# A decoder layer on one core: x pairs and squares ordered on two engines, the last gate chains cut into parts, four summed loads issued earlier

## The chip, the cores and the metric

The kernel runs on one core of a Trainium2 chip. The metric is the device time of one execution in microseconds (us), as the median of several. Five engines work side by side, each through its own list of instructions in order: PE (TensorE, matmuls; its weight loads are shown as PEld), DVE (VectorE), ACT (ScalarE), POOL (GpSimd) and SP (SyncE, which here only issues DMA transfers). They wait for each other through semaphores. PE accumulates in PSUM, which has eight banks of 128 x 512 float32.

## The reference

One layer of a decoder on x of 256 tokens by 2048, all in float32. A Griffin branch and a stick-breaking attention run in parallel from the same normed input, are gated and summed; a SwiGLU feed-forward of 5632 and a gated embedding follow.

```
h = rmsnorm(x, g_mix)
x_r, g_r, q, k, v, gate_r, gate_a = split(h @ w_in)       # 2816, 2816, then 5 x 2048
xc = causal_depthwise_conv(x_r)                           # width 4
r, i = sigmoid(xc @ w_rg_a + b_a), sigmoid(xc @ w_rg_x + b_x)   # 16 diagonal blocks of 176
a = exp(-8 * r * softplus(-lam));  u = sqrt(1 - a*a) * (i * xc)
hh[t] = a[t] * hh[t-1] + u[t]                             # scan along tokens
y_r = (gelu(g_r) * hh) @ w_rnn_out
y_a = stick_breaking_attention(headnorm(q), headnorm(k), v) @ w_attn_out
x = x + (sigmoid(gate_r) * y_r + sigmoid(gate_a) * y_a) @ w_o
g, u = split(rmsnorm(x, g_ffn) @ w_ffn_gu);  x = x + (silu(g) * u) @ w_ffn_down
x = x + sigmoid(rmsnorm(x, g_ple) @ w_ple_gate) * (p @ w_ple_proj)
```

## The kernel before

**Weights as a stream.** All weights lie packed in one array in the order of use. A plan lists 128 x 128 tiles by stage; `CHUNKS` cuts it into chunks of up to eight tiles (128 x 1024, 512 KB). Here w5, whi 5 and wlo 5 are the raw load and the two halves of chunk 5, numbered from 0 over the whole plan. `Stream.dma_to` issues a chunk's load on SP into one of four `p32` buffers. `Stream.split_to` makes two float32r halves: `whi` on ACT (a copy, L277), then `wlo` on DVE (weight minus whi, L278), each in one of four buffers. So a load waits for the split of the chunk four before it, and a split waits for PE to be done with the chunk four before it. Each float32 product is three matmuls, high x high, high x low, low x high: `prod` (L546 to L548) for token-major results, `mm3` (L458 to L460) for the block-diagonal gates, `wide`/`low` (L476, L480) for feature-major ones. A chunk in `prod` is 12 matmuls of 512 columns.

**Summed chunks.** In some groups (`group`) seven products stand for eight on 2 x 2 blocks. Their slots have string names. "11", "T1", "21" and "22" are loaded into tiles with the tag Q (26 of 128 x 1024) instead of `p32`; `summed` (L261, DVE) adds them in place for "T1" to "T4". The order of the recurrent output's group ("ro", 0) is `LONG`: 11, T1, 21, 4, 5, 22, 6, 7, 8, T2, and so on; these are chunks 142 to 151.

**Order.** A scheduler orders each engine's list from the program, dependences and priorities. `tc.issue_after(ins)` puts what is traced inside behind `ins` on the engine of `ins`, and on no other.

**Stages around the change.** (1) Head: eight x pairs (two 128-row tiles of x transposed each) are loaded; `norm_parts` scales each by g_mix and splits it (ACT then DVE, two of each, 128x256; L357 and L354); `norm_sq` squares it on ACT and adds into `acc0` on DVE. Beside this runs the first group, half of gate_r, from w_in. `later` ties both to the DVE split (`lo_ins`). (2) Recurrence: for p = 0 to 10, `rnn_g(p)` computes a pair of columns of g_r and its gelu, `rnn_conv` a pair of x_r, `rnn_gates(p)` the block-diagonal products and then a chain: two sigmoids, exp and tanh, sqrt, the scan and a split of y. Sigmoid, gelu, exp/tanh and sqrt need different function tables on ACT, each change one ACT_TABLE_LOAD. `decay_scales` computes per-channel constants, within p = 0. After p = 9 and p = 10 (`GATE_R_AT`) follows one `block` of gate_r, eight chunks, and its two sigmoids (`gate`). L800 then loads the table with log and exp. (3) The recurrent output ("ro", two groups), v, attention and the rest follow. (4) At the end ("pg", two groups) `embedded(g)` makes four products of p in PSUM, which wait in their banks for the sigmoid of the gate; the last part writes the output.

Of the kernel before, what the change touches and what calls it, by code (L numbers as in the profile page):

```python
# [2 lines left out]

# [7 lines left out]
AF = mybir.ActivationFunctionType  # L11
# [15 lines left out]
NPR = KR // 2  # L27
NPD = KD // 2
# [7 lines left out]
LONG = ["11", "T1", "21", 4, 5, "22", 6, 7, 8, "T2", 9, 10, 11, "T3", 12, 13, 14, "T4", 15, 16, 17, 18, 19, 20, 21]  # L36
TWO = (0, 1)
LAST_GROUP = ("pg", 1)
NEG = -1e30


def pairs_of(name):

    return (0, 1, 2) if name == "gu" else (0, 1)


def is_sum(x):

    return isinstance(x, str) or isinstance(x, tuple) and x[0] == "S"
# [14 lines left out]
C_XR, C_GR, C_Q, C_K, C_V, C_GTR, C_GTA = 0, 22, 44, 60, 76, 92, 108  # L64
# [17 lines left out]
GATE_R_AT = {9: 2, 10: 3}  # L82
# [95 lines left out]
PLAN = plan()  # L178
# [9 lines left out]
CHUNKS = []  # L188
# [9 lines left out]
    LAST.append(len(CHUNKS))  # L198


class Stream:


# [5 lines left out]
        self.raw, self.parts, self.after = {}, {}, {}  # L209

    def dma_to(self, n):
        n = min(n, len(CHUNKS))
        while self.n_dma < n:
            j = self.n_dma
            i, a, b = CHUNKS[j]
            c = P * (b - a)
            mode = PLAN[i][0][3] if PLAN[i][0][0] == "tok" else 0
            if is_sum(mode):
                if c:
                    t = self.quad()  # L220
                    self.raw[mode] = t
            else:
                t = self.p32.tile([P, 1024], F32, tag="w32", name=f"w32_{j}")
                self.raw[j] = t
            if c:
                src = self.w[OFFS[j]:OFFS[j] + P * c].rearrange("(p c) -> p c", p=P)
                self.nc.sync.dma_start(t[:, :c], src)
            self.n_dma += 1
            if j in self.after:
                self.after.pop(j)()  # L230
# [93 lines left out]
def tile_hybrid_block(ctx: ExitStack, tc: tile.TileContext, xT: bass.AP, x: bass.AP, pT: bass.AP,  # L324
                      prm: bass.AP, w: bass.AP, out: bass.AP):
    nc = tc.nc
# [10 lines left out]
    def tl(tag, dt=F32):  # L337
        cnt[0] += 1
        tag = "H" if tag in "CT" else "Q"
        n, c = NT[tag]  # L340
        return act.tile([P, c], dt, tag=tag, name=f"{tag}_{cnt[0]}", bufs=n)
# [8 lines left out]
    def tt(o, a, b, op):  # L350
        nc.vector.tensor_tensor(o, a, b, op)  # L351
# [4 lines left out]
    def actv(o, i, f, **kw):  # L356
        nc.scalar.activation(o, i, f, **kw)  # L357

    S_ = Stream(nc, w, p32, phl, lambda: tl("X"), 4, 3)
# [25 lines left out]
    def pc(base, j):  # L385
        return prm_sb[:, base + j:base + j + 1]
# [13 lines left out]
    for n in ("h", "l"):  # L400
        t = cst.tile([P, 512], F32R, tag=f"w1{n}", name=f"w1{n}")
# [138 lines left out]
    def tok(pairs, k, t):  # L540
        x = rhs(pairs, k)
        return x[:, t * P:t * P + P], x[:, 256 + t * P:384 + t * P]

    def prod(ps, x, wh, wl, start=False, stop=False, goes_on=False):

        nc.tensor.matmul(ps, x[0], wh, start=start, stop=False, skip_group_check=goes_on)  # L546
        nc.tensor.matmul(ps, x[0], wl, start=False, stop=False, skip_group_check=goes_on)  # L547
        nc.tensor.matmul(ps, x[1], wh, start=False, stop=stop, skip_group_check=goes_on)  # L548
# [118 lines left out]
    xc, xcs, gel, y, gtr, ysum, xsum = {}, {}, {}, [], [], {}, {}  # L667
# [26 lines left out]

    def rnn_g(p):
        g = from_x(C_GR, p, "T")
        actv(g, g, AF.Gelu_apprx_tanh)
        gel[p] = g

    def rnn_gates(p):  # L700
        i = S_.pos
        wts = S_.take(("rg", p))
        wts = [wts[x] for x in range(wts.n)]
        if PLAN[i + 1][0] == ("rg2", p):
            w2 = S_.take(("rg2", p))
            wts += [w2[x] for x in range(w2.n)]
        n = 0
        pss = []
        for _ in range(2):
            ps = psum()  # L710
            for e in range(2):
                ks = rg_k_tiles(2 * p + e)
                for x, k in enumerate(ks):
                    t = rhs(xcs, k)
                    mm3(ps[:, e * 256:e * 256 + 256], wts[n], t[:, :256], t[:, 256:], x == 0,
                        x == len(ks) - 1)
                    n += 1
            pss.append(ps)
        r, i_, a = tl("T"), tl("T"), tl("T")
        for e in range(2):  # L720
            s = slice(e * 256, e * 256 + 256)
            actv(r[:, s], pss[0][:, s], AF.Sigmoid, bias=pc(PC_BA, 2 * p + e))
        for e in range(2):
            s = slice(e * 256, e * 256 + 256)
            actv(i_[:, s], pss[1][:, s], AF.Sigmoid, bias=pc(PC_BX, 2 * p + e))
        for e in range(2):
            s = slice(e * 256, e * 256 + 256)
            actv(a[:, s], r[:, s], AF.Exp, scale=cA[:, 2 * p + e:2 * p + e + 1])
        for e in range(2):
            s = slice(e * 256, e * 256 + 256)  # L730
            actv(r[:, s], r[:, s], AF.Tanh, scale=cT[:, 2 * p + e:2 * p + e + 1])
        nc.vector.tensor_scalar(r, r, -1.0, 1e-30, ALU.mult, ALU.max)
        actv(r, r, AF.Sqrt)
        tt(i_, i_, xc[p], ALU.mult)
        stt(r, a, 1.0, r, ALU.add, ALU.mult)
        tt(i_, i_, r, ALU.mult)
        for e in range(2):
            s = slice(e * 256, e * 256 + 256)
            nc.vector.tensor_tensor_scan(r[:, s], a[:, s], i_[:, s], 0.0, ALU.mult, ALU.add)
        tt(r, r, gel[p], ALU.mult)  # L740
        y.append(split(r, "B"))
        if p in pairs_of("ro"):
            ysum[p] = half_sums(r)

    def block(c0, b, step=None):

        pss = [psum() for _ in range(2)]
        wt = S_.take(("blk", c0, b))
        for k in range(KD):
            if step is not None and k % 2 == 0:  # L750
                step()
            _, _, hi, lo, o = wt[4 * k]
            for t, ps in enumerate(pss):
                prod(ps, tok(xg, k, t), hi[:, o:o + 512], lo[:, o:o + 512], k == 0, k == KD - 1)
        return pss
# [1 line left out]
    def rs_x(t):  # L757
        return rstd_tok[:, t:t + 1]

    def gate(c0, b, tag, step=None):  # L760
        ts = [tl(tag) for _ in range(2)]
        for t, ps in enumerate(block(c0, b, step)):
            actv(ts[t], ps, AF.Sigmoid, scale=rs_x(t))
        return ts


    def later(f):

        def run():
            with tc.issue_after(S_.lo_ins.ins):  # L770
                f()
        return run

    def squares_x(i):
        return later(lambda: norm_sq(xt[i], acc0, i == 0))

    also = {2 * i - 3: later(next_xg) for i in range(2, NPD)}
    also.update({n: squares_x(i) for i, n in enumerate((2, 4, 6, 8, 10, 12, 13, 14))})
    pss = group(("gtr", 0), xg, None, None, also)[0]

    def scaled_gates():
# [6 lines left out]
    for p in range(2):  # L788
        rnn_conv(p, from_x(C_XR, p, "T", scaled_gates if p == 0 else None, scale=False))
    for p in range(NPR):  # L790
        rnn_g(p)
        if p + 2 < NPR:
            rnn_conv(p + 2, from_x(C_XR, p + 2, "T", scale=False))
        if p == 0:
            with tc.issue_after(S_.lo_ins.ins):
                decay_scales()
        rnn_gates(p)
        if p in GATE_R_AT:
            gtr.append(gate(C_GTR, GATE_R_AT[p], "C"))
    tc.keep_in_program_order(nc.scalar.preload_act_table_set("natural_log_exp_and_others"))  # L800

    def whole(at, pairs, sums, also=()):

# [8 lines left out]
    def xg_sums(p):  # L812
        h = tl("T")
        hi, lo = parts(xg[p])
        tt(pair(h), f32(hi), f32(lo), ALU.add)
        xsum[p] = half_sums(h)

    n = len(LONG)
    for g in range(2):
        also = {n - 2 + i: (lambda p: lambda: xg_sums(p))(p) for i, p in enumerate(pairs_of("v"))} if g else ()  # L820
        for i, c in enumerate(whole(("ro", g), y, ysum, also)):
            o = gtr[2 * g + i // 2][i % 2]
            tt(o, c, o, ALU.mult)
# [3 lines left out]
    for g in range(2):  # L827
        for i, c in enumerate(whole(("v", g), xg, xsum)):
            r = rs_x(i % 2)
            v = tl("B", F32R)  # L830
# [117 lines left out]
    at = {}  # L948
# [5 lines left out]
    def step():  # L954
        for f, hp in at.pop(slot[0], ()):
            f(hp)
        slot[0] += 1
# [27 lines left out]
    for g in range(2):  # L985
        for i, ps in enumerate(group(("ao", g), ost, None)[0]):
            c, m = gta[2 * g + i // 2][i % 2], mix_r[2 * g + i // 2][i % 2]
# [46 lines left out]
    for g in range(2):  # L1034
# [11 lines left out]
        for n, ps in enumerate(group(("wo", g), mix, msum, fold)[0]):  # L1046
            t, b = n % 2, 2 * g + n // 2
# [53 lines left out]
    def embedded(g):  # L1101
        def run():
            for b in range(2):
                w_ = S_.take(("tok", "pg", g, ("x", b)))[0]
                for t in range(2):
                    ps = psum()
                    for k in range(2):
                        s = slice(k * 512, k * 512 + 512)
                        prod(ps, tok(pts, k, t), w_[2][:, s], w_[3][:, s], k == 0, k == 1)
                    pp.append(ps)  # L1110
        return run

    for g in range(2):
        qs_, t_ = group(("pg", g), h3, sum3, also={len(SEVEN) - 3: embedded(g)})
        for n, (q, c, op) in enumerate(zip(qs_, ("11", "T3", "T1", "T3"), (ALU.add,) * 3 + (ALU.subtract,))):
            t, b = n % 2, 2 * g + n // 2
            c, ps, o = t_[c], pp.pop(0), tl("T")
            m = 512 if g == 0 or n < 3 else 256
# [69 lines left out]
```

## Time and profile before

| | us |
|---|---|
| median of 3 runs | 1893.24 (1893.03 to 1894.4) |
| profiled execution | 1895.76 |
| its span, first to last instruction | 1894.0 |
| first matmul of the stream / last matmul starts | 5.36 / 1885.66 |

The profile is of one execution. "Busy" counts an engine's instructions; matmuls are pipelined and their ends are modelled, so 0.39 us is shown for a matmul whose successor starts 0.227 us later. "Idle before <- X" names what ended an idle time. A line of the code can be a helper's, so L277, L278, L351, L354 and L357 stand for many places. The stretches around the change:

| stretch | us | PE busy | DVE busy | ACT busy | granted clock |
|---|---|---|---|---|---|
| head | 8 to 21 | 12.04 | 6.46 | 12.07 | 1.00 |
| head, on | 21 to 26 | 3.76 | 3.59 | 5.00 | 1.00 |
| block after p = 9 | 340 to 356 | 15.01 | 11.43 | 12.68 | 1.00 |
| gates and block of p = 10 | 356 to 394 | 38.00 | 20.96 | 25.76 | 1.00 |
| start of the recurrent output | 394 to 416 | 18.42 | 15.71 | 14.54 | 0.92 |
| attention to the last group but one | 450 to 1825 | 1375.00 | 1000.52 | 791.58 | 1.00 |
| middle of the last stage | 1825 to 1845 | 19.65 | 16.49 | 13.27 | 1.00 |

### The profile page before, as it was taken

Reading aid. Unit: us, or ns where it says so; the run is one execution under the profiler, and the core shown is the slowest. Engines: PE = TensorE matmul, PEld = TensorE weight load, DVE = VectorE, ACT = ScalarE, POOL = GpSimd, SP = SyncE. Lnnn points to the kernel's source line nnn. Section 1 sums busy time; section 2 is a strip of 40 time slices with the busy share of each in tenths; the row PEclk is TensorE's granted clock in tenths of the full one; section 3 lists DMA queues with packets and bytes.
Section 4 is the critical chain, followed back from the end, with each engine's and each line's share of the span. In section 5 each row is a group of like instructions: output and inputs, shape, how many; then the busy total and the mean of one; then the engine's idle time right before and its main releaser. Section 6 shows DMA issues by size and latency. Waiting matters only on the chain.

```text
span 1894.0 us, 24003 instructions
## 1 busy us (share of the span) xinstructions
PE 1877.4 (99%) x9000; PEld 1575.7 (83%) x9000; DVE 1378.1 (73%) x1649; ACT 1156.7 (61%) x1531; POOL 2.2 (0%) x9
## 2 busy tenths in 40 slices
PE   9999999999999999999999999999999999999998
PEld 7899989878888888888888888888888888888886
DVE  6688887666786566665578988866886688855776
ACT  6688888764455567666455766544664466543663
POOL 0000000000000000000000000000000000000000
PEclk9999999999999999999999999999999999999999
DMA  7556555565646654555666555476447646466554
GB/s 268 180 177 195 196 175 193 182 221 179 232 146 190 199 162 146 171 169 166 193 217 215 201 214 220 144 255 213 161 160 254 213 146 221 147 220 190 171 191 138
DMA packets 101925, 361.36 MB, mean 191 GB/s; under 512 B 11440, under 2 KB 12080, under 8 KB 101808
## 3 DMA queue, kind: packets, MB, share of 16 engines
q1 hardware_dynamic: 101664, 359.82, 56.9%
q8 instruction: 70, 1.15, 0.3%
q14 instruction: 47, 0.39, 0.1%
q10 hardware_dynamic: 144, 0.01, 0.0%
HBM read 357.69 MB, written 2.10 MB: 190 GB/s over the span
## 4 chain that ended last, share of the span: by engine, by line
PE 95%; ACT 2%; DVE 1%; DMA 1%; issue 1%; SPq 0%; DVEq 0%; ACTq 0%
PE ps L547 26%; PE ps L548 26%; PE ps L546 26%; PE ps L476 8%; PE ps L480 4%; PE ps L459 1%; PE ps L460 1%; PE ps L458 1%; ACT L357 1%; ACT H L357 1%; DMA w<-in_w_dram 1%; ACT whi L277 1%; PE ps L1071 1%; DVE wlo L278 0%; DVE H L351 0%
## 5 line engine op out<-in xcount | busy, mean ns | idle before, releaser
L278 DVE TENSOR_TENSOR wlo<-w,whi 128x1024 fp32r<-128x1024 f32 (+1 forms) x580 | 701.2, 1215 | 375.7 <-ACT whi L277 370.9
L277 ACT ACTIVATE whi<-w 128x1024 fp32r<-128x1024 f32 (+1 forms) x580 | 607.1, 1052 | 469.3 <-PE ps L548 410.6
L547 PE MATMUL ps<-wlo,Q 128*128 128x512 f32 x2223 | 867.9, 390 | 1.4 <-DVE wlo L278 1.3
L548 PE MATMUL ps<-whi,Q 128*128 128x512 f32 x2223 | 866.8, 390 | 0.0
L546 PE MATMUL ps<-whi,Q 128*128 128x512 f32 x2223 | 791.5, 392 | 5.7 <-ACT whi L277 5.3
L546 PEld LDWEIGHTS ps<-whi,Q 128*128 128x128 f32 x2223 | 416.7, 188 | 93.3 <-ACT whi L277 8.5
L547 PEld LDWEIGHTS ps<-wlo,Q 128*128 128x128 f32 x2223 | 417.8, 188 | 89.8 <-DVE wlo L278 4.8
L548 PEld LDWEIGHTS ps<-whi,Q 128*128 128x128 f32 x2223 | 417.7, 188 | 86.7
L277 ACT ACTIVATE whi<-Q 128x1024 fp32r<-128x1024 f32 (+1 forms) x177 | 182.5, 1032 | 137.3 <-PE ps L548 114.5
L278 DVE TENSOR_TENSOR wlo<-Q,whi 128x1024 fp32r<-128x1024 f32 (+1 forms) x177 | 210.2, 1189 | 53.4 <-ACT whi L277 53.2
L476 PE MATMUL ps<-Q,whi 128*128 128x512 f32 x704 | 170.7, 392 | 0.0
L476 PEld LDWEIGHTS ps<-Q,whi 128*128 128x128 f32 x704 | 128.8, 188 | 24.5
L351 DVE TENSOR_TENSOR H<-ps,H 128x512 f32<-128x512 f32 (+1 forms) x170 | 98.4, 609 | 25.2 <-PE ps L548 16.0
L261 DVE TENSOR_TENSOR Q<-Q,Q 128x1024 f32<-128x1024 f32 x76 | 92.8, 1221 | 1.2 <-DMA Q<-in_w_dram 0.3
L480 PEld LDWEIGHTS ps<-Q,wlo 128*128 128x128 f32 x704 | 90.4, 191 | 3.5
L480 PE MATMUL ps<-Q,wlo 128*128 128x256 f32 x704 | 91.5, 283 | 0.0
L357 ACT ACTIVATE H<-ps 128x512 f32<-128x512 f32 (+1 forms) x122 | 60.4, 516 | 48.0 <-PE ps L548 28.4
L357 ACT ACT_TABLE_LOAD x64 | 82.1, 1283 | 1.1
L351 DVE TENSOR_TENSOR H<-H,H 128x512 f32<-128x512 f32 (+2 forms) x107 | 63.3, 598 | 3.1 <-ACT H L357 2.6
L357 ACT ACTIVATE Q<-H 128x512 fp32r<-128x512 f32 x41 | 25.1, 625 | 26.5 <-DVE H L351 25.6
L460 PE MATMUL ps<-Q,wlo 128*128 128x256 f32 x140 | 39.6, 283 | 0.0
L459 PE MATMUL ps<-Q,whi 128*128 128x256 f32 x140 | 39.6, 283 | 0.0
(130 smaller groups left out, 855.0 us busy)
## 6 DMA issues: line engine op xcount, KB each, us to landing
w<-in_w_dram SPq DMA_DIRECT2D x558, 512.0 KB, 3.9
Q<-in_w_dram SPq DMA_DIRECT2D x98, 512.0 KB, 6.1
w<-in_w_dram SPq DMA_DIRECT2D x16, 448.0 KB, 3.3
H<-in_x_dram SPq DMA_DIRECT2D x8, 256.0 KB, 5.3
H<-in_xT_dram SPq DMA_DIRECT2D x7, 256.0 KB, 7.6
out_dram<-H SPq DMA_DIRECT2D x7, 256.0 KB, 5.1
w<-in_w_dram SPq DMA_DIRECT2D x4, 320.0 KB, 3.4
w<-in_w_dram SPq DMA_DIRECT2D x2, 256.0 KB, 3.0
```

The costliest lines, as they stand in the source:

```text
L261: self.nc.vector.tensor_tensor(r[o], r[o], r[a], ALU.add)
L277: self.hi_ins = self.nc.scalar.activation(hi[:, :c], t[:, :c], AF.Copy)
L278: self.lo_ins = self.nc.vector.tensor_tensor(lo[:, :c], t[:, :c], hi[:, :c].bitcast(F32), ALU.subtract)
L351: nc.vector.tensor_tensor(o, a, b, op)
L357: nc.scalar.activation(o, i, f, **kw)
L459: nc.tensor.matmul(o, wt[0], xl, start=False, stop=False)
L460: nc.tensor.matmul(o, wt[1], xh, start=False, stop=stop)
L476: nc.tensor.matmul(pss[e], wt[0], rhs(xs, k), start=(k == 0), stop=(k == n - 1))
L480: nc.tensor.matmul(pss[e][:, :256], wt[1], rhs(xs, k)[:, :256], start=False, stop=False)
L546: nc.tensor.matmul(ps, x[0], wh, start=start, stop=False, skip_group_check=goes_on)
L547: nc.tensor.matmul(ps, x[0], wl, start=False, stop=False, skip_group_check=goes_on)
L548: nc.tensor.matmul(ps, x[1], wh, start=False, stop=stop, skip_group_check=goes_on)
```

## The change

- `dma_order` sorts the issue of loads: a summed chunk of ("ro", 0) gets a place 4.5 chunks ahead of its own in the plan, and `DMA_UPTO` makes a request for n chunks include them.
- `later` becomes `behind_splits`: what is traced inside stands behind the latest whi split on ACT and the latest wlo split on DVE. It also holds `decay_scales`. The x pair and square are requested at other slots, mostly by turns.
- `rnn_gates` becomes a generator with four stops. For p = 9 and 10 its parts are traced before chunks 0, 2, 4 and 5 of the eight chunks of the following block (`count`), behind the splits and behind the gelu.
- The sigmoids of the last block go to slot 8 of ("ro", 0) (`last_gate`), the table load to slot 12 (`next_table`), both behind the splits.
- The four products of p for the first half of "pg" are copied by ACT from PSUM to SBUF.

```diff
+EARLY = {("ro", 0): 4}
...
+def dma_order():
+
+    def key(j):
+        k = PLAN[CHUNKS[j][0]][0]
+        early = k[0] == "tok" and is_sum(k[3]) and k[1:3] in EARLY
+        return j - (EARLY[k[1:3]] + 0.5 if early else 0)
+    order = sorted(range(len(CHUNKS)), key=key)
+    at = {j: n for n, j in enumerate(order)}
+    upto, m = [0], 0
+    for j in range(len(CHUNKS)):
+        m = max(m, at[j] + 1)
+        upto.append(m)
+    return order, upto
...
-        n = min(n, len(CHUNKS))
+        n = DMA_UPTO[min(n, len(CHUNKS))]
         while self.n_dma < n:
-            j = self.n_dma
+            j = DMA_ORDER[self.n_dma]
...
+        yield
         for e in range(2):
...
+    @contextmanager
+    def behind_splits():
+        with tc.issue_after(S_.hi_ins.ins), tc.issue_after(S_.lo_ins.ins):
+            yield
...
-            with tc.issue_after(S_.lo_ins.ins):
+            with behind_splits():
                 f()
...
-    also = {2 * i - 3: later(next_xg) for i in range(2, NPD)}
-    also.update({n: squares_x(i) for i, n in enumerate((2, 4, 6, 8, 10, 12, 13, 14))})
+    also = {max(1, 2 * i - 4): [later(next_xg)] for i in range(2, NPD)}
+    for i in range(NPD):
+        also.setdefault(2 * i + 1 if i < 7 else 14, []).append(squares_x(i))
...
-        rnn_gates(p)
-        if p in GATE_R_AT:
-            gtr.append(gate(C_GTR, GATE_R_AT[p], "C"))
-    tc.keep_in_program_order(nc.scalar.preload_act_table_set("natural_log_exp_and_others"))
+        parts_ = rnn_gates(p)
+        next(parts_)
+        if p not in GATE_R_AT:
+            list(parts_)
+            continue
+
+        count = [0]
+
+        def step():
+            if count[0] in (0, 2, 4, 5):
+                with behind_splits(), tc.issue_after(gelu.ins):
+                    next(parts_, None)
+            count[0] += 1
+
+        pss = block(C_GTR, GATE_R_AT[p], step)
+        if p < NPR - 1:
+            gtr.append(sigmoids(pss, "C"))
+        else:
+            pend_gtr = pss
...
+    def last_gate():
+        with behind_splits():
+            gtr.append(sigmoids(pend_gtr, "C"))
+
+    def next_table():
+        with behind_splits():
+            nc.scalar.preload_act_table_set("natural_log_exp_and_others")
...
-        also = {n - 2 + i: (lambda p: lambda: xg_sums(p))(p) for i, p in enumerate(pairs_of("v"))} if g else ()
+        also = {n - 2 + i: (lambda p: lambda: xg_sums(p))(p) for i, p in enumerate(pairs_of("v"))} if g else {
+            8: last_gate, 12: next_table}
...
+                    if g == 0:
+                        t_ = tl("T")
+                        actv(t_, ps, AF.Copy)
+                        ps = t_
                     pp.append(ps)
```

## The prediction

> **What bounds the kernel.** I read the page's busy times first, then who waited for whom on PE, the table of stretches, and last the timelines of PE, ACT and DVE where PE waited.
>
> ```profile
> span 1894.0 us, 24003 instructions
> ...
> PE 1877.4 (99%) x9000; PEld 1575.7 (83%) x9000; DVE 1378.1 (73%) x1649; ACT 1156.7 (61%) x1531; POOL 2.2 (0%) x9
> ```
>
> PE is the bound. The diff leaves the number of matmuls at 9000, so only time in which PE waits or runs slowly can be won. The waits on PE:
>
> ```profile
> PE ps L546 <- ACT whi L277: 5.3, 5, 1.8
> PE ps L588 <- DVE ones_r L398: 1.5, 1, 1.5
> PE ps L547 <- DVE wlo L278: 1.3, 3, 0.8
> PE ps L546 <- DVE H L351: 0.3, 1, 0.3
> ```
>
> Few, and all for a weight chunk's two halves (whi by ACT, wlo by DVE) or for DVE. A busy sum hides half of the loss, because a matmul's modelled 0.39 us overlaps the next. I therefore count from start to start: undisturbed 512-column matmuls start 0.227 us apart (408.57, 408.80, 409.03 in PE's timeline), a full chunk of 12 takes 2.72. Four places fall behind this.
>
> Head, ACT's timeline (start, length, operation):
>
> ```profile
> 15.81 0.89 ACT L357 ACTIVATE Q<-H,gm_sb 128x256 fp32r<-128x256 f32 x2
> 16.60 0.62 ACT L357 ACTIVATE H<-H 128x512 f32<-128x512 f32 x1
> ...
> 20.57 0.61 ACT L357 ACTIVATE H<-H 128x512 f32<-128x512 f32 x1
> 21.09 1.04 ACT L277 ACTIVATE whi<-w 128x1024 fp32r<-128x1024 f32 x1
> ```
>
> Four x pairs and squares in a row hold the next whi back to 21.09, though its weights landed at 18.70. Gate chain of p=9, PE's timeline:
>
> ```profile
> 345.44 0.42 PE L546 MATMUL ps<-whi,Q 128*128 128x512 f32 x1
> 346.62 0.50 PE L547 MATMUL ps<-wlo,Q 128*128 128x512 f32 x1 [0.76 <-DVE wlo L278]
> ```
>
> Start of the recurrent output, ACT, then PE:
>
> ```profile
> 392.71 1.06 ACT L277 ACTIVATE whi<-Q 128x1024 fp32r<-128x1024 f32 x1 [2.52 <-DMA Q<-in_w_dram]
> 396.40 2.01 ACT L277 ACTIVATE whi<-Q 128x1024 fp32r<-128x1024 f32 x2 [2.63 <-DVE Q L261]
> 398.42 1.28 ACT L357 ACT_TABLE_LOAD   x1
> 399.72 1.27 ACT L357 ACTIVATE H<-ps,rstd_tok 128x512 f32<-128x512 f32 x2
> 401.00 1.28 ACT L800 ACT_TABLE_LOAD   x1
> 402.30 1.06 ACT L277 ACTIVATE whi<-w 128x1024 fp32r<-128x1024 f32 x1
> ```
>
> ```profile
> 403.41 0.97 PE L546 MATMUL ps<-whi,Q 128*128 128x512 f32 x3 [1.83 <-ACT whi L277]
> ```
>
> The summed load lands late, and then the last gate's sigmoids with two table loads stand between two splits. Right after, the granted clock halves (stretch, PE, PEld, DVE, ACT, POOL, clock, DMA share, GB/s):
>
> ```profile
> 394.00:416.00 22.00, 18.42 (x69) 13.44 (x68) 15.71 (x14) 14.54 (x16) 0.00 (x0) 0.92 0.61 211
> 404.50:407.90 3.40, 3.23 (x8) 2.56 (x9) 2.99 (x4) 2.66 (x4) 0.00 (x0) 0.50 0.61 177
> ```
>
> Tail, PE:
>
> ```profile
> 1839.52 0.47 PE L546 MATMUL ps<-whi,Q 128*128 128x512 f32 x1 [0.35 <-DVE H L351]
> ```
>
> **x pairs and squares: -2.0.** The two chunks from 17.91 to 25.39 take 7.48 for 2 x 2.72 = 5.44: 2.04 lost. In the changed program's order each pair and square stands behind a split on ACT as well as on DVE. Walked with these rows: w4 lands 13.43, whi to 14.5; pair 2 to 15.35; the first square to 15.87; whi of w5 to 16.8 (0.9 later than before), its wlo to 18.1, wanted by PE at 18.83. Pair 3 to 17.6; w6, no longer behind the load of pair 6 (0.65 us at the 1.3 us per 512 KB of these landings), lands at 18.05, whi to 19.1, wlo (behind pair 3's low half) to 20.4; PE wants them at 20.6 and 21.5. Afterwards ACT needs per two chunks 2 x 0.95 + 0.8 + 0.6 = 3.3 us of PE's 5.44, DVE 3.8. The loads of pairs 6 and 7 move behind w9 and w10 on SP: about 23 and 25, asked for by ACT past 27 and 32. The wait for w2 near 8 us is the DMA's and stays.
>
> The decay scales' Abs and Exp leave the head and bring a table load of their own, 1.28 us. It lands in this hole of ACT, which it fits with its two 0.2 us neighbours:
>
> ```profile
> 98.27 0.66 ACT L357 ACTIVATE H<-ps 128x256 f32<-128x256 f32 x2 [2.42 <-PE ps L476]
> ```
>
> I take 0; were there no cover, the next whi (98.81, wanted by PE at 104.56) still has over 3 us. The Trainium skill, "ScalarE: Activation LUTs", section "What ACT_TABLE_LOAD costs", adds a drain of about 1.38 us to each load. Here the instruction behind a load starts 0.01 later (402.29 to 402.30), and with the drain the hole would overflow by 0.6, still under PE's cover. The total of loads stays 66 (p=9 saves one).
>
> **Chains of p=9 and p=10 in four parts: -2.0.** First matmuls of the gate's chunks stand at 342.72, 345.44, 349.27, 352.56 and 355.61; the last three steps are 3.83, 3.29 and 3.05 for 2.72: 2.01 lost. Before, whi of the chunk due at 345.44 ended at 345.31, behind four table loads. Now gelu comes first (no return to its table) and splits stand between parts: whi 339.8 to 340.85, wlo to 342.1; the following ones end whi 344.8, 345.8, 348.65 and wlo 346.05, 347.2, 350.3, for starts at 347.9, 350.6, 353.4. Delayed y is split at 352.9, used far later. Nothing waits.
>
> **Summed loads moved up, last sigmoids and table moved down: -6.7.** From the group's first matmul (394.84) to its eighth chunk (415.15) lie 60 matmuls (chunks 11, T1, 21, 4, 5, 22, 6): 20.31 for 13.6. What p=10's chain delays shows here too. The walk, as if the earlier savings had not shifted it: the four Q loads now issue behind w131; their buffers' last readers are gate matmuls of p=6 to p=9, done by 334.5, so SP does not stop. They add 4 x 1.3 = 5.2 us of transfer ahead of w132 to w134, landing about 359 to 362 (shifted by the 2 us of p=9), wanted by whi at about 359 to 364.5 because the split buffers free up only then. PE's margin over the finished splits: some 4 us. I charge 0.
>
> whi 11 then runs 386.8 to 387.9 instead of 392.71; DVE, solid from 390.4: wlo 11, y's low half, two sums (1.22 each), wlo T1 to 395.7, wlo 21 to 396.9, a third sum, wlo 4 to 399.2. PE asks for these at 396.4, 397.6 and 399.4; ACT's whi T1, 21, 4, 5 end 394.5, 395.4, 396.4, 398.0 for 396.0, 396.2, 398.7, 400.7. So covered, but by 0.2 to 0.7 only. The sigmoids (1.28 + 1.27) now follow the split of the eleventh chunk and the table load that of the fifteenth, where ACT is more than a chunk ahead; they hold two of eight PSUM banks and the group takes five. Bounds of this term: at least 3.9 (the 398.42 to 402.30 block leaves, loads late as before), at most 6.7.
>
> **Copies of the embedded products: -0.5.** Four ACT copies (0.58 each) near 1826 to 1830, where ACT's next split is wanted 7 us later; they free the bank for which PE lost 1839.52 - 1838.79 - 0.23 = 0.5. The end after the last matmul (1885.66 to 1894.02) keeps its order: 0.
>
> **Sum:** 2.0 + 2.0 + 6.7 + 0.5 = 11.2 against the profile's span of 1894.0 (1895.76 with what lies around it). That execution is 2.5 above the median of 1893.24; the waits are in both, so I take it off the median: 1882.0, and leave 0.5 for DVE's thin margin: **1882.5**.
>
> **Rivals.**
> 1. *The half clock does not belong to the waits and stays*: eight matmuls at 0.427 instead of 0.227, about 1.7 back: 1884.2. For: PE's longest idle before it is 1.83 us. Against: it is the only one after the warm-up, right behind the only cluster of waits. The Trainium skill, "TensorE: Matmul & The Clock Gate", Part 1, wants an idle window of about 3.4 us before the clock halves, which speaks for this rival; the trace shows no such idle, yet the clock fell.
> 2. *The loads do not land earlier, or DVE takes ACT's place*: only 3.9 of 6.7: 1893.24 - 8.4 = 1884.8. DVE's 0.2 us margin speaks for it, the free buffers against it.
> 3. *Given back elsewhere*: head and p=9 return their 4 (the late wlo of w5, say) and the output keeps 3.9: 4.4 left, 1888.8; a little more and it is no change.
> 4. *Slower: the four early loads starve the gates of p=10.* Eight loads follow w131 up to w135, four of them moved. If each took the 4.4 us that w131 took from issue to landing, one after another, w135 would land at 353.9 + 35.2 and be split 2.3 later for a PE that wants it at 373.6: 17.8 lost, net 6.6 slower, 1899.8. It outweighs the gains from (17.4 + 11.2) / 8 = 3.6 us per load. Against: five loads in a row landed 1.3 us apart at 392.6 to 397.7, and SP had free time.
>
> **Chances.** Forecast 0.60, rival 1 0.13, rival 2 0.13, rival 3 0.08 (half of it within 0.2%), rival 4 0.06. Runs of this kernel tell 0.2%, 3.8 us, from no change. The first three reach to 1885, rival 3 adds some: 1880.7 to 1887. Faster 0.90, same 0.04, slower 0.06.
>
> **What would show it.** Head: no ACT wait near 20; chunks 2.72 apart from 12 on. Gates: none near 345. Output: Q landed by 362, no table load between the splits of 21 and 4, seven chunks in about 13.6, granted clock 1.00. Tail: no wait for DVE H. Wrong if PE waits for wlo at the output's start, for w between 355 and 375, or anywhere new.

## The result, and the profile after

The changed kernel takes 1883.88 us, median of 4 runs (1883.51 to 1884.7), against 1893.82 for the kernel before beside it (1893.03 to 1895.63). The ratio is 0.9947, 95% interval 0.993 to 0.9964: 9.9 us less. The forecast was 1882.5 in 1880.7 to 1887.0. The profiled execution took 1884.7, its span fell from 1894.0 to 1883.0.

The waits on PE, changed kernel (engine and line that waited, who ended the wait: total, times, longest, in us):

```profile
PE ps L607 <- DVE ones_r L417: 1.5, 1, 1.5
```

Three of the four rows are gone. What stays is the start, before the stream's first matmul. (Lines have moved: L277 is now L296, L278 L297, L261 L280, L546 to L548 L565 to L567, and L357 L376.) The stretches, with the columns of the table before:

```profile
340.00:356.00 16.00, 16.00 (x72) 13.27 (x71) 12.00 (x15) 13.28 (x18) 0.00 (x0) 1.00 0.73 266
394.00:416.00 22.00, 22.00 (x99) 18.23 (x98) 15.67 (x15) 14.62 (x17) 0.00 (x0) 1.00 0.72 239
```

The start of the recurrent output held 69 matmuls in 22 us, now 99 do, at a clock of 1.00 for 0.92. ACT's timeline in the head and then at the recurrent output:

```profile
18.02 1.06 ACT L296 ACTIVATE whi<-w 128x1024 fp32r<-128x1024 f32 x1 [0.43 <-DMA w<-in_w_dram]
18.99 0.62 ACT L376 ACTIVATE H<-H 128x512 f32<-128x512 f32 x1
19.51 1.05 ACT L296 ACTIVATE whi<-w 128x1024 fp32r<-128x1024 f32 x1
20.46 0.89 ACT L376 ACTIVATE Q<-H,gm_sb 128x256 fp32r<-128x256 f32 x2
21.26 1.04 ACT L296 ACTIVATE whi<-w 128x1024 fp32r<-128x1024 f32 x1
```

```profile
383.04 1.06 ACT L296 ACTIVATE whi<-Q 128x1024 fp32r<-128x1024 f32 x1
...
389.63 2.01 ACT L296 ACTIVATE whi<-Q 128x1024 fp32r<-128x1024 f32 x2 [2.32 <-DVE Q L280]
391.55 1.04 ACT L296 ACTIVATE whi<-w 128x1024 fp32r<-128x1024 f32 x1
...
404.80 1.06 ACT L296 ACTIVATE whi<-w 128x1024 fp32r<-128x1024 f32 x1 [0.98 <-PE ps L567]
405.88 1.28 ACT L376 ACT_TABLE_LOAD   x1
407.17 1.27 ACT L376 ACTIVATE H<-ps,rstd_tok 128x512 f32<-128x512 f32 x2
```

In the head a pair or a square stands between two splits, never four of each. At the output the split of 11 is done at 384.10, 6.9 before PE starts that chunk at 391.00. The sigmoids stand where ACT is ahead.

PE place by place in the two profiled executions (the first row is a point in time, the next two are lengths, the last is time over the pace):

| place | before | after | gain | forecast |
|---|---|---|---|---|
| head: first matmul of chunk 7 at | 25.39 | 23.57 | 1.82 | 2.0 |
| chunks 124 to 131 (p = 9) | 23.794 | 21.787 | 2.01 | 2.0 |
| chunks 142 to 148 (recurrent output) | 20.31 | 13.60 | 6.71 | 6.7 |
| the wait for DVE near the end | 0.50 | 0 | 0.50 | 0.5 |

These sum to 11.04; the last matmul starts 11.01 earlier. Outside these places PE takes the same time in both to within 0.04 us.

### The profile page after: what moved, and what is told of

It reads as the page before. It is cut to its first block, busy times and chain, and to the rows that moved or that the text cites. A ratio compares the mean times of both kernels' runs of the same rounds, so it can differ in the third digit from the quotient of the medians.

```text
span 1883.0 us, 24009 instructions
## 1 busy us (share of the span) xinstructions
PE 1873.4 (99%) x9000; PEld 1576.0 (84%) x9000; DVE 1377.9 (73%) x1649; ACT 1158.5 (62%) x1535; POOL 2.2 (0%) x9
## 4 chain that ended last, share of the span: by engine, by line
PE 99%; DMA 0%; DVE 0%; SPq 0%; ACT 0%; issue 0%; DVEq 0%
PE ps L567 27%; PE ps L566 27%; PE ps L565 27%; PE ps L495 9%; PE ps L499 4%; PE ps L479 1%; PE ps L478 1%; PE ps L477 1%; PE ps L1127 1%; DMA w<-in_w_dram 0%; PE ps L919 0%; PE ps L1068 0%; DVE H L370 0%; PE ps L1030 0%; PE ps L973 0%; PE ps L972 0%
## 5 line engine op out<-in xcount | busy, mean ns | idle before, releaser
L297 DVE TENSOR_TENSOR wlo<-w,whi 128x1024 fp32r<-128x1024 f32 (+1 forms) x580 | 701.1, 1215 | 370.1 <-ACT whi L296 365.2
L296 ACT ACTIVATE whi<-w 128x1024 fp32r<-128x1024 f32 (+1 forms) x580 | 607.4, 1052 | 461.9 <-PE ps L567 402.4
L567 PE MATMUL ps<-whi,Q 128*128 128x512 f32 x2223 | 866.0, 390 | 0.0
L565 PE MATMUL ps<-whi,Q 128*128 128x512 f32 x2223 | 792.5, 392 | 0.0
L567 PEld LDWEIGHTS ps<-whi,Q 128*128 128x128 f32 x2223 | 417.4, 188 | 86.6
L565 PEld LDWEIGHTS ps<-whi,Q 128*128 128x128 f32 x2223 | 417.0, 188 | 85.5 <-ACT whi L296 0.8
L296 ACT ACTIVATE whi<-Q 128x1024 fp32r<-128x1024 f32 (+1 forms) x177 | 182.6, 1032 | 132.2 <-PE ps L567 112.3
L297 DVE TENSOR_TENSOR wlo<-Q,whi 128x1024 fp32r<-128x1024 f32 (+1 forms) x177 | 210.1, 1189 | 50.3 <-ACT whi L296 50.1
L280 DVE TENSOR_TENSOR Q<-Q,Q 128x1024 f32<-128x1024 f32 x76 | 92.8, 1221 | 0.9
L376 ACT ACTIVATE H<-ps 128x512 f32<-128x512 f32 (+1 forms) x126 | 62.7, 518 | 48.1 <-PE ps L567 30.1
L376 ACT ACTIVATE Q<-H 128x512 fp32r<-128x512 f32 x41 | 25.1, 625 | 26.2 <-DVE H L370 25.5
```

What stands on the lines that cost most here:

```text
L280: self.nc.vector.tensor_tensor(r[o], r[o], r[a], ALU.add)
L296: self.hi_ins = self.nc.scalar.activation(hi[:, :c], t[:, :c], AF.Copy)
L297: self.lo_ins = self.nc.vector.tensor_tensor(lo[:, :c], t[:, :c], hi[:, :c].bitcast(F32), ALU.subtract)
```

## The experiments

Kernels of one group ran on one chip beside the kernel before. The changed kernel was not run again beside them, and the kernel before took 1894.48, 1894.02 and 1894.42 there, 0.2 to 0.7 more than beside the changed kernel. So a difference from the changed kernel is uncertain by about that much; what PE loses at a place, read from a trace, is not. "Lost at the output" is the time from the first matmul of chunk 142 to that of chunk 149, less 13.6.

**The old head.**

```diff
-            with behind_splits():
+            with tc.issue_after(S_.lo_ins.ins):
                 f()
...
+    also = {2 * i - 3: later(next_xg) for i in range(2, NPD)}
+    also.update({n: squares_x(i) for i, n in enumerate((2, 4, 6, 8, 10, 12, 13, 14))})
```

> The changed kernel with the old head: x pairs, squares and decay scales tied to DVE's split alone and asked for at the old slots. Theory of the prediction: a whi split again stands behind two pairs and two squares, PE waits near 20, and the time is 1.8 longer than the changed kernel's (first 50 us lose 5.4 over 0.227 us a matmul instead of 3.6). Rival: with the rest of the change in place the time is given back before 300 us: within 0.5 of the changed kernel.

1886.88 (1886.38 to 1887.16), ratio 0.9962 [0.9947, 0.9976]: 3.0 longer than the changed kernel, or 2.3 when each is taken against the kernel before beside it; 1.8 was expected. ACT again does four pairs and four squares between two splits (14.69 to 19.98), and PE is 1.2 over its pace at 19.67. So the gain is the head's, and the rival falls. Its size scatters. Over the first 50 us, the three profiles with the old head lose 5.4, 4.2 and 4.3, the eleven with the new tie 2.7 to 3.6, 3.1 in the mean: 1.6 apart. Not all of the longer time is the head's: in the profiled execution 9.3 lie between the last matmul's start and the end, for 8.3 in the changed kernel, because the last output takes 3.4 from issue to landing, for 2.4.

**The old slots, but both ties.**

```diff
+    also = {2 * i - 3: later(next_xg) for i in range(2, NPD)}
+    also.update({n: squares_x(i) for i, n in enumerate((2, 4, 6, 8, 10, 12, 13, 14))})
```

> The changed kernel with the old slots of x pairs and squares, but still tied to both splits. Theory: the tie to ACT's split is what counts, a pair and a square stand between two whi splits either way: within 0.5 of the changed kernel, no wait of PE on ACT near 20. Rival: the slots count, since a pair and a square that are asked for in the same slot meet the split of the next chunk: the 3.0 of the old head come back.

1884.37 (1884.27 to 1884.67), ratio 0.9948 [0.9931, 0.9964], as the changed kernel, with no wait near 20. What acts is the tie to ACT's split; the slots are worth nothing that shows here.

**Chains whole, loads back, sigmoids back.** Each undoes one part.

```diff
+        list(parts_)
         if p not in GATE_R_AT:
-            list(parts_)
             continue
...
-        pss = block(C_GTR, GATE_R_AT[p], step)
+        pss = block(C_GTR, GATE_R_AT[p])
```

> The changed kernel with the gate chains of p = 9 and p = 10 in one piece, ahead of their blocks. Theory of the prediction: 2.0 longer, all of it between 340 and 356, and the start of the recurrent output as in the changed kernel. Rival: the uncut chain of p = 10 also changes which Q buffer the load of the summed block 22 gets; it then waits for p = 10's gate matmuls and issues behind w148, lands near 392, and DVE's sum that reads it stands ahead of the low half of T1: another 2 to 3 at the start of the recurrent output, 4 to 5 in all.

1886.97 (1886.56 to 1887.21): 3.1 longer. Chunks 124 to 131 take 23.77 for 21.79, the 2.0 forecast. Lost at the output: 0.88. The load of 22 does issue behind w148, but it lands in time: DVE's two sums run through from 389.73. PE waits once, 0.75, for the low half of 21. So the rival's order held and its price did not.

```diff
-EARLY = {("ro", 0): 4}
+EARLY = {}
```

> The changed kernel without the new order of loads (EARLY is empty). Theory of the prediction: the four summed loads go back, 2.8 longer (6.7 less the 3.9 of the sigmoids). Rival 1: in the order of instructions three of the four loads stay where they are, behind w131, and only that of 22 moves, behind w149; if it lands near 392.6, DVE's second sum, which reads it and stands ahead of the low half of T1 (391.95 before, wanted by PE at 392.59), is 3 late: 2.5 to 3.5 longer, by one load and one sum. Rival 2: the loads are hidden and nothing changes: within 0.5.

1884.2 (1883.73 to 1884.4), ratio 0.9947 [0.993, 0.9964]: no change. The prediction's 2.8 fails, and so does the rival's 3. DVE's timeline:

```profile
387.71 1.22 DVE L280 TENSOR_TENSOR Q<-Q,Q 128x1024 f32<-128x1024 f32 x1
389.42 1.23 DVE L280 TENSOR_TENSOR Q<-Q,Q 128x1024 f32<-128x1024 f32 x1 [0.50 <-DMA Q<-in_w_dram]
390.57 2.35 DVE L297 TENSOR_TENSOR wlo<-Q,whi 128x1024 fp32r<-128x1024 f32 x2
```

The second sum waits 0.50 for the load of 22, PE loses 0.21. The other three loads issue at 348.29 to 349.23, behind w131, though nothing orders them early any more.

```diff
-        if p < NPR - 1:
-            gtr.append(sigmoids(pss, "C"))
-        else:
-            pend_gtr = pss
+        gtr.append(sigmoids(pss, "C"))
+    tc.keep_in_program_order(nc.scalar.preload_act_table_set("natural_log_exp_and_others"))
```

> The changed kernel with the last gate's two sigmoids and the log/exp table traced at their old place, right behind the block. They then stand on ACT between whi of 21 and whi of 4: 1.28 + 1.27 + 1.28 = 3.83. Theory of the prediction: 3.9 longer. Rival 1: ACT is ahead there by now, so part is hidden: whi of 4 ends 391.64 + 3.83 + 1.05 = 396.5 where PE wants it at 394.85, and its low half follows: 2.0 longer, clock 1.00. Rival 2: the same wait brings the half clock back: 2.0 + 1.7 = 3.7, with a granted clock of 0.5 for about 3.4 us behind it.

1887.78 (1886.33 to 1888.4): 3.9 longer, 3.88 lost at the output. PE's timeline and two stretches of 3.41 us:

```profile
393.98 0.39 PE L567 MATMUL ps<-whi,Q 128*128 128x512 f32 x1
395.76 0.96 PE L565 MATMUL ps<-whi,Q 128*128 128x512 f32 x3 [1.39 <-ACT whi L296]
397.02 0.64 PE L566 MATMUL ps<-wlo,Q 128*128 128x512 f32 x1 [0.30 <-DVE wlo L297]
```

```profile
393.81:397.22 3.41, 1.72 (x7) 0.82 (x6) 1.27 (x2) 3.40 (x5) 0.00 (x0) 1.00 0.00 0
397.22:400.63 3.41, 3.41 (x9) 2.63 (x9) 3.20 (x3) 2.30 (x3) 0.00 (x0) 0.50 0.63 184
```

Some 2.3 are waits; eight matmuls at 0.427 for 0.227, 1.6, make the rest. The forecast's 3.9 came out, but by rival 2's mechanism: part of the 3.83 is hidden, and the half clock fills it up. It need not come each time. One stretch of 3.41 us at half clock takes 0.0009 off an execution's mean granted clock, and of the five executions two (1886.33 and 1886.74) have a mean of 0.999 and three (1887.78 to 1888.4, the profiled one among them) 0.998. So the two shorter ones probably had no half clock, which is rival 1's case.

**Chains and loads back together; the new order alone.** The first carries both edits above. The second is the kernel before with `dma_order` and its two uses, nothing else.

> The changed kernel with both the gate chains whole again and the new order of loads empty. In the order of instructions the four summed loads now stand behind w148, as in the kernel before. Theory A (the cut of the chains and the new order each move the loads up by themselves, so undoing one shows nothing): the loads land near 390 to 396, and beside the 2.0 of p = 9 another 2 to 3 are lost at the start of the recurrent output: 4 to 5 longer than the changed kernel, about 1 to 2 longer than with the chains alone whole (3.1). Theory B (the place of the loads is worth nothing once the sigmoids are gone from there): as with the chains alone whole, 1887.

> The kernel before with the new order of loads alone (its old head, whole chains, early sigmoids, no copies). In the order of instructions the loads of 11, T1 and 21 stand behind w129, that of 22 still behind w148. Theory A: 2.8 to 3.2 shorter than the kernel before (6.7 less the 3.9 or the 3.5 of the sigmoids), about 1891, with the rest of the loss at the split of 4 behind the sigmoids. Theory C (ACT's two tables and sigmoids set the time of that place by themselves): within 1 of the kernel before.

The first: 1889.88 (1888.48 to 1890.82), 6.0 longer than the changed kernel and 2.9 longer than with the chains alone whole; 4.53 lost at the output, with the half clock (six matmuls at 0.427 from 397.8). The four loads stand behind w148 and the split of 11 waits for its load again:

```profile
390.92 1.06 ACT L296 ACTIVATE whi<-Q 128x1024 fp32r<-128x1024 f32 x1 [3.00 <-DMA Q<-in_w_dram]
394.62 2.00 ACT L296 ACTIVATE whi<-Q 128x1024 fp32r<-128x1024 f32 x2 [2.63 <-DVE Q L280]
```

The second: 1890.52 (1890.3 to 1891.2), ratio 0.9981 [0.9972, 0.9991], 3.5 shorter than the kernel before; 2.59 lost at the output for 6.71, no half clock. Theory A's mechanism holds in both, and B and C fall; its sizes were short: 4 to 5 longer for 6.0 in the first, where it left out the half clock, and 2.8 to 3.2 shorter for 3.5 in the second. All kernels with their places:

| chains cut | new order | sigmoids late | where the loads stand on SP | lost at the output | half clock |
|---|---|---|---|---|---|
| yes | yes | yes | four behind w131 | 0.00 | no |
| yes | no | yes | three behind w131 | 0.21 | no |
| no | yes | yes | three behind w129 | 0.88 | no |
| no | yes | no | three behind w129 | 2.59 | no |
| yes | yes | no | four behind w131 | 3.88 | yes |
| no | no | yes | all behind w148 | 4.53 | yes |
| no | no | no | all behind w148 | 6.71 | yes |

Either edit alone moves the loads up; undoing both brings the stall back. (Rows 4 and 7 have the old head.)

**The loads twice.**

```diff
-                self.nc.sync.dma_start(t[:, :c], src)
+                [self.nc.sync.dma_start(t[:, :c], src) for _ in range(1 + (j in (142, 143, 144, 147)))]
```

> The changed kernel with each of the four early summed loads (11, T1, 21, 22) issued twice into the same tile: four more transfers of 512 KB stand among w132 to w135 on SP. Theory of the prediction (a load costs 1.2 to 1.3 of transfer, PE's cover is some 4, by the changed kernel's landings 5.5 to 6): w133 to w135 land 5 later and nothing or at most 1 is lost. Rival 4 of the prediction (a load costs 4.4 from issue to landing, one behind another, with 3.6 a load as its point): 17 later and 11 or more lost, from chunk 132 on.

1884.69 (1883.84 to 1885.79), ratio 0.995 [0.9935, 0.9965]. The loads land some 1.3 apart, w133 at 359.6, w134 at 363.5, w135 at 366.0 (359.3, 360.6 and 361.8 in the changed kernel, where w131 issues 0.9 later), and PE waits for none. So w135 comes 5.1 later, as forecast. Rival 4 falls: with eight loads for four there is still cover. PE does lose 0.23 at the start of the output, at the low half of 4, where DVE has only 0.18 to spare in the changed kernel.

**Stalls of chosen length.** A whi split is written several times, for example:

```diff
-            self.hi_ins = self.nc.scalar.activation(hi[:, :c], t[:, :c], AF.Copy)
+            for _ in range({484: 7, 491: 7, 498: 7, 573: 6, 580: 8, 587: 8}.get(j, 1)):
+                self.hi_ins = self.nc.scalar.activation(hi[:, :c], t[:, :c], AF.Copy)
```

> The changed kernel with six of its whi splits in the feed-forward written 10, 12, 14 (chunks 484, 491, 498) and 11, 13, 15 times (573, 580, 587) on ACT, to stall PE once at each: about 0.8 to 6 us, growing with the number, in stretches where it loses nothing. Rule of an idle window (PE has to stand idle for the whole of some 3.4 us): stalls under that leave the pace at 0.227 us a matmul, longer ones bring 0.427 for 3.4 us. Rule of a share (as before the change, where of 401.2 to 404.6 PE waited 2.8 with a longest wait of 1.83): stalls from about 2 to 3 us on bring it, by where the window falls. Half clock that has nothing to do with waits: none at any.

> As the run with stalls, with whi written 7, 7, 7 times (chunks 484, 491, 498) and 6, 8, 8 times (573, 580, 587). By 1.05 a copy from the first run, PE should wait some 2.6, 1.9, 2.9, 1.4, 3.9 and 4.0. Rule of an idle window (3.4 us wholly idle): only the last two can halve the clock. Rule of a share (the clock halves when PE starts five or fewer of the 15 matmuls that 3.4 us have room for; six did not halve it at 20 us and at 396 in other runs): waits from about 2.2 on halve it in some positions of the window, 1.4 and 1.9 in none.

The first run's stalls came out far too long (5.7 to 11.2 over the pace, 1947.46 in all); each was followed by the pace of 0.427, for 2.1 to 5.1 us. It settles only that waits bring it. The second run (1908.64; each of the two is a single execution) has five; that of 573 left none. Over the pace they took 2.42, 2.70, 2.52, 3.61 and 3.61, and all but the third were followed by the half clock. The half clock begins at 1253.93, 1277.82, 1482.62 and 1506.52: these points lie 7, 60 and 7 times 3.413 us apart, so the clock changes on a grid that runs on by itself. The first and the third stall, PE's timeline, then the windows of that grid around them:

```profile
1252.16 1.21 PE L566 MATMUL ps<-whi,Q 128*128 128x512 f32 x4 [2.25 <-ACT whi L297]
...
1299.47 1.20 PE L566 MATMUL ps<-whi,Q 128*128 128x512 f32 x4 [2.36 <-ACT whi L297]
```

```profile
1250.52:1253.93 3.41, 1.72 (x6) 1.14 (x7) 2.48 (x3) 1.59 (x3) 0.00 (x0) 1.00 0.46 187
1253.93:1257.34 3.41, 3.41 (x9) 2.68 (x9) 3.41 (x4) 0.41 (x1) 0.00 (x0) 0.50 0.79 269
1294.89:1298.30 3.41, 2.22 (x10) 1.50 (x8) 0.00 (x0) 3.38 (x4) 0.00 (x0) 1.00 0.05 20
1298.30:1301.72 3.42, 2.19 (x8) 1.53 (x9) 2.27 (x2) 1.11 (x2) 0.00 (x0) 1.00 0.49 162
```

The wait of 2.25 leaves six starts in one window of the grid, and the next window runs at half clock. The wait of 2.36 is cut in two by the end of a window; nine matmuls start in the first part's window and eight in the second's, and the clock stays. No wholly idle 3.4 us is needed.

**No copies.**

```diff
-                    if g == 0:
-                        t_ = tl("T")
-                        actv(t_, ps, AF.Copy)
-                        ps = t_
```

> The changed kernel without the four ACT copies of the embedded products. Theory of the prediction: PE waits once for DVE near 1828, as it did at 1838.79, 0.5 longer. Rival: nothing, as that wait came only from where the work stood in time: within 0.2 in PE's starts.

1884.49 (1884.38 to 1884.84), ratio 0.9951 [0.9936, 0.9966]. PE waits once, 0.51 over its pace, at 1827.51. The term is right to the tenth, and the wait did not come from where the work stood in time.

**The end on GpSimd**, an attempt at a shorter kernel.

```diff
-                tt(o[:, s], o[:, s], x1[t][b][:, s], ALU.add)
+                (nc.gpsimd if g and n < 3 else nc.vector).tensor_tensor(o[:, s], o[:, s], x1[t][b][:, s], ALU.add)
```

> The changed kernel with three of the last additions of x (128x512, 0.68 each on DVE at 1874.83, 1876.36 and 1877.30) on GpSimd. DVE is busy without a break from 1874.8 to 1879.3 and its last result goes out 3.7 before the end. If DVE bounds the end: 1.3 to 2.0 shorter, last matmul to end 6.4 to 7.1 instead of 8.4. Rival: GpSimd takes longer than 1.5 for one and its transfers become the last: no gain or a loss.

1884.22 (1883.95 to 1884.65), ratio 0.9947 [0.9932, 0.9962]: no gain. The last additions of DVE in the changed kernel, then GpSimd and DVE in this one (DVE's second addition shows in a window of its own):

```profile
1878.56 0.75 DVE L370 TENSOR_TENSOR H<-H,H 128x256 f32<-128x256 f32 x2
```

```profile
1874.10 3.72 POOL L1184 TENSOR_TENSOR H<-H,H 128x512 f32<-128x512 f32 x3 [1868.13 <-DVE H L370]
...
1876.04 0.82 DVE L370 TENSOR_TENSOR H<-ps,H 128x256 f32<-128x256 f32 x2 [0.24 <-ACT H L376]
1876.78 1.31 DVE L1184 TENSOR_TENSOR H<-H,H 128x256 f32<-128x256 f32 x1
...
1878.02 0.41 DVE L1184 TENSOR_TENSOR H<-H,H 128x256 f32<-128x256 f32 x1
```

GpSimd takes 1.24 for one, so the rival's reason (longer than 1.5) is not it. DVE's addition that starts beside the last of them takes 1.31 and ends 0.27 behind it; the next, with GpSimd idle, takes 0.41 as in the changed kernel. DVE is done 4.2 after the last matmul's start, for 4.7, yet the last output is issued 4.8 after it in both: SP now issues the last three one right behind the other (1878.13, 1878.51, 1879.03). So DVE does not bound the end alone. From last matmul to end it is 8.3 as before. No version was found that beats the changed kernel.

## Why the prediction was right, and where it was not

**Head, 2.0.** 1.82 between the profiles, 1.6 between the means of several, 3.0 between the medians (2.3 against the kernels before beside them). The mechanism is right, and its cause is the tie to ACT's split alone: the two chunks that took 7.48 now take 5.44 (18.13 to 23.57), the whole 2.04, and ACT's walk came out to 0.1 (whi of w5 done at 16.8, of w6 at 19.1). The other 0.2 went ahead of these chunks. One number is a coincidence: the wait for w2 "stays", I wrote; in the after profile it is 0.1 instead of 0.9, because PE ran at half pace until 6.8 instead of 5.1 and was late itself. That is four matmuls, 0.8, which cancels it.

**Chains, 2.0.** 2.01, and 1.99 when undone. Right.

**Output, 6.7.** The sum is right, 6.71, and so is the walk: the split of 11 began at 383.04, 3.8 before the 386.8 of a walk that left out the earlier savings of 1.8 and 2.0; DVE's margins, forecast at 0.2 to 0.7, are 0.64 (low half of T1 done 391.95, wanted 392.59), 0.64 and 0.18. What failed is how I divided it. First, "at least 3.9 (the 398.42 to 402.30 block leaves, loads late as before)": with the loads at their old place the late sigmoids save only 6.71 - 4.53 = 2.18: the block is 3.9 long, but PE waited only 2.1 for the split behind it. The waits for the late loads stay (some 3.2 of the 4.53), and they bring the half clock (1.3) by themselves. Second, I gave the other 2.8 to the new order of loads. In the kernel with chains cut the order is worth 0.21; in the kernel before, 4.12. The cut of the chains moves three of the loads up by itself, which the diff does not say and the order of instructions of a kernel with that edit alone does. Third, the parts do not add: each of the three rows with loss above 3 has the half clock in it, 1.2 to 1.6.

**Copies, 0.5.** Right, shown by taking them away.

**From the sum to the time.** 11.2 was taken off the median of 1893.24, though it was read from an execution of 1895.76. The spans of the kernel before run from 1891.2 to 1894.1 in the 34 executions beside the experiments, so the profiled one, 1894.0, was among the longest. Against its own time the sum gives 1895.76 - 11.2 = 1884.6; the profiled execution after took 1884.7. The medians fell by 9.94, 1.1 less than the 11.04 between the two profiles. That step, not a term, was wrong. The 1.4 between 1882.5 and 1883.88 are this 1.1, the 0.6 by which the kernel before came out above 1893.24 beside the changed one, and 0.2 of the sum, less the 0.5 kept back for DVE's margin, which cost nothing there. That the forecast came so near is in part luck. What makes the long executions of the kernel before long stays open, as only one was traced. That the half clock is missing in the short ones is not likely: all 34 have a mean granted clock of 0.998, whereas 36 of 42 executions of the kernels whose profile shows no half clock behind the start have 0.999.

**Rivals.** The first (half clock stays) falls: it comes with the waits and left with them. The second (loads not earlier, or DVE in ACT's place) falls, with 0.18 to spare in one place. The third (given back elsewhere) falls: no wait is new, and the last matmul moved by the sum. The fourth falls by the loads issued twice. The moved Abs and Exp cost nothing: from chunk 7 to the block of p = 9 PE takes 309.14 before and 309.13 after.

## What to carry to other kernels

Undo parts in pairs as well as one by one: two edits that each suffice for the same effect look worthless when only one is taken away. Where an order comes from a scheduler, compare the order of instructions for each edit by itself before a gain is given to one of them. And take a sum off the time of the execution in which it was read, not off a median that may not hold the same losses.

## What the runs showed of the hardware

The half clock needs no idle window. In each of the fourteen traces the granted clock changes only at whole multiples of 3.413 us from its first change. On that grid, PE started five matmuls or fewer in 26 windows that ran at full clock, those at the kernels' ends included, and half clock followed on each of them. It followed on one of the two windows with six, and on none of those with eight or more (no window had seven). The waits of at most 1.39 us (sigmoids back) and 1.0 (chains and loads back) left five starts each of the 15 that a window holds. All of this fits a limit on the share of starts in a window that runs on by itself, somewhere between five and eight of 15, and where the grid cuts a wait then decides whether half clock follows, as it did for the wait of 2.25 and did not for that of 2.36. The Trainium skill, "TensorE: Matmul & The Clock Gate", Part 1, names one idle window of about 3.4 us as the condition. These runs disagree with "idle"; they agree with its free-running window, as the grid shows, and with its cold pace (426.7 ns for 512 columns; 427 here).

The same page of the Trainium skill says that the warm-up varies between runs. Here the half pace at the start ended anywhere from 4.2 to 7.2 us, 5 to 12 matmuls at 0.2 each: 1.0 to 2.4 us that scatter from one execution to the next and belong to no edit.

A DVE addition of two SBUF tiles of 128x256 took 1.31 beside a busy GpSimd and 0.41 without it, so work moved to GpSimd came back on DVE in part. Two additions of a PSUM and an SBUF tile beside the busy GpSimd kept their pace (0.82 for both). The Trainium skill, "GPSIMD Engine Reference", section "1. Specifications", says that GpSimd shares its SBUF interface with VectorE and contends with VectorE's instructions that read two SBUF inputs; these rows agree.
